# The prompt's layer-0 SwiGLU as seven block products, its moving operands streamed from DRAM through a ring

## The chip, the cores and the metric

The kernel runs on one core of one Trainium2 chip. The metric is device time of one execution in microseconds (us). The engines are TensorE (PE: matmuls, with the weight loads as a row of their own, PEld), VectorE (DVE), ScalarE (ACT), GpSimd (POOL) and SyncE (SP), which issues nearly all DMAs of this kernel from one queue, in order.

## The reference

Two residual layers run over two sequences, a prompt of 1024 tokens and a sample of 512, with the same weights. Layer 0 mixes tokens by a grouped Fourier transform, layer 1 by grouped-query attention (8 query heads, 2 key/value heads of 128); each is followed by a SwiGLU.

```python
def swiglu_ffn(x, g, w_gate, w_up, w_down):
    h = rms_norm(x, g)
    return (jax.nn.silu(h @ w_gate) * (h @ w_up)) @ w_down

def run_trunk(x):
    cos, sin = axial_rope_tables(x.shape[1])
    for i in range(DEPTH):                       # DEPTH = 2
        j = i // 2
        if i % 2 == 0:
            x = x + fourier_mixer(x, norm_mix[i], fourier_w[j])
        else:
            x = x + attention_mixer(x, norm_mix[i], attn_w_qkv[j], attn_q_norm[j],
                                    attn_k_norm[j], attn_w_o[j], cos, sin)
        x = x + swiglu_ffn(x, norm_ffn[i], ffn_w_gate[i], ffn_w_up[i], ffn_w_down[i])
    return x
```

The model width is 1024, the hidden width of the SwiGLU 2816. All is float32.

## The kernel before

Tokens are cut into three blocks of 512: block 0 is the sample, blocks 1 and 2 the prompt. Activations are kept transposed: a block is 8 chunks `dc` of 128 features by 512 tokens. Each float32 operand of a large product is split into a high part that TensorE multiplies exactly and a low rest, and `mm3` issues three matmuls for one product (high x high, high x low, low x high; lines 247, 248 and 249). ACT makes the high part (`act.copy`, a cast), VectorE or GpSimd the low one by a subtraction (`split`, lines 240 and 241; `weights`, lines 278 and 279). Residuals rest in DRAM (`xres`).

`ffn(layer, b, h)` is the SwiGLU of one block: for each of 22 chunks `fc` of the hidden width, 8 products for gate, 8 for up (into two `g` banks of PSUM), then silu, product and split into `mid`, and 8 products of the down projection, held in `pend` and issued one by one among the next chunk's. A down product goes to one of two `c` banks, and VectorE adds it to the accumulator (`acc`, line 750).

`ffn_pair(layer, blocks, ops, outs)` is the SwiGLU of two blocks at once, before the change for layer 1 only. Per pass it takes two hidden chunks f0 and f1, two halves of the contraction and two blocks, a 2x2 by 2x2 block product for gate and up, by seven block products and additions instead of eight (11 passes). A block product is 24 matmuls (two banks, gate and up; four feature chunks; three matmuls). Its stationary operands, sums and differences of weight blocks, come from `operands`/`stationary` (GpSimd adds at lines 924 to 930, then a split), its seven moving operands (B11, B21, T2, T1, B22, T3, N4: sums and differences of the normalised blocks) from `moving`. Five of these lie in SBUF (pool `mT`), two go to DRAM (`late`) and come back once into the slot `hA` before the pair needs them. Product banks: two tiles of two banks (`gT`, shown as `a`) and the two `g` banks, in turn. `plus` (line 915), `silu` and `hidden` empty them; 32 down products per pass go through `pend`.

`weave(main, main_cost, aux, aux_cost)` sets the order in which code is written out: a main stream (F) and an auxiliary one (X) are generators that yield costs, and the one that is behind in its share of its cost goes on; `lead` steps of the main stream come first. A scheduler then orders the instructions of each engine by that priority and by what it takes to be ready. Slots of tiles are given by tag (`BUFS`). The stages before, main and auxiliary:

1. `ffn(0, 0)` beside the prompt's Fourier mixer, its projection, and the norm of block 1
2. `ffn(0, 1)` beside the sample's attention (`qkv(0)`, `attend((0,))`) and the norm of block 2
3. `ffn(0, 2)` beside the sample's output projection, `qkv(1)`, and the norm of block 0
4. `ffn(1, 0)` beside `qkv(2)`, `attend((1, 2))`, two output projections and `moving`
5. `ffn_pair(1, (1, 2))` alone

## Time and profile before

| | |
|---|---|
| three runs | 3037.09 us median, 3036.11 to 3038.55 |
| profiled execution | span 3039.1 us, which is the time the profile gives for it |
| TensorE | 2965.8 us busy (98%), 14,184 matmuls |
| VectorE, ScalarE, GpSimd | 1660.7, 1235.4, 1283.2 us busy |
| DMA | 330.05 MB, mean 109 GB/s |
| mean granted TensorE clock | 0.995 of full speed |

Of these stages, 1 runs to about 530 us, 2 to 1043, 3 to 1533, 4 to 2350 and 5 to the end. A matmul's bar in the profile is longer than the distance to the next start, since matmuls overlap; what one costs is read from the starts, or from the number of matmuls in a window. Idle time counts only on TensorE or where it ends in a wait of TensorE. Tile names in the profile lack their digits: `B`, `T` and `late` are the moving operands, `a`, `g` and `c` PSUM banks.

### The profile page before, as it was taken

How to read it: one execution, taken by the hardware profiler on the slowest of the kernel's cores; microseconds unless marked ns; L12 is line 12 of the kernel's file. 1: busy time of each engine (PE TensorE's matmuls, PEld its weight loads, DVE VectorE, ACT ScalarE, POOL GpSimd, SP SyncE). 2: the span in 40 equal slices, each digit the busy share in tenths (PEclk: the TensorE clock that was granted, in tenths of full speed). 3: DMA queues.
4: the chain of work that ended last, by engine and by line, in shares of the span. 5: the costliest groups of instructions: out<-in, count | busy, mean ns of one | idle time of the engine just before them, and what ended most of it. 6: DMA issues, size and time to landing. Idle time of an engine off the chain costs nothing. (4 is left out here: it accounts for less than half of the span.)

```text
span 3039.1 us, 36901 instructions
## 1 busy us (share of the span) xinstructions
PE 2965.8 (98%) x14184; PEld 2434.2 (80%) x14184; DVE 1660.7 (55%) x2875; ACT 1235.4 (41%) x1843; POOL 1283.2 (42%) x652
## 2 busy tenths in 40 slices
PE   7999999999999999999999999999999999999999
PEld 6778888888877788888878788877787787887777
DVE  6785565534555543533473465665236555655566
ACT  6443232433466522333343577776324222222221
POOL 4434444433333644444433311313636644644452
PEclk9999999999999999999999999999999999999999
DMA  7434543332322734433343211212635411111111
GB/s 228 146 111 149 167 133 93 128 101 84 97 91 94 237 127 133 141 104 101 102 141 108 86 57 53 80 46 91 222 122 183 163 56 55 43 56 56 44 54 63
DMA packets 132080, 330.05 MB, mean 109 GB/s; under 512 B 14176, under 2 KB 28512, under 8 KB 131264
## 3 DMA queue, kind: packets, MB, share of 16 engines
q1 hardware_dynamic: 130688, 318.71, 32.2%
q0 software_dynamic: 928, 7.94, 0.7%
q8 instruction: 111, 1.82, 0.2%
q10 hardware_dynamic: 288, 1.05, 0.1%
q14 instruction: 65, 0.53, 0.1%
HBM read 280.45 MB, written 47.19 MB: 108 GB/s over the span
## 5 line engine op out<-in xcount | busy, mean ns | idle before, releaser
L279 POOL TENSOR_TENSOR w<-raw,w 128x1024 fp32r<-128x1024 f32 x354 | 847.5, 2405 | 1308.2 <-ACT w L278 1225.1
L750 DVE TENSOR_TENSOR acc<-c,acc 128x512 f32<-128x512 f32 x704 | 483.1, 689 | 443.4 <-PE c L249 439.1
L278 ACT CAST w<-raw 128x1024 fp32r<-128x1024 f32 x354 | 371.0, 1049 | 561.7 <-PE c L249 271.7
L247 PE MATMUL g<-h,w 128*128 128x512 f32 x1408 | 556.2, 395 | 3.6 <-ACT t L782 3.6
L249 PE MATMUL g<-h,w 128*128 128x512 f32 x1408 | 552.2, 392 | 0.5 <-POOL w L279 0.5
L248 PE MATMUL g<-h,w 128*128 128x512 f32 x1408 | 552.2, 392 | 0.0
L247 PE MATMUL c<-mid,w 128*128 128x512 f32 x1056 | 417.7, 397 | 15.5 <-DVE acc L750 10.8
L248 PE MATMUL c<-mid,w 128*128 128x512 f32 x1056 | 414.3, 392 | 1.7 <-DVE mid L241 1.7
L249 PE MATMUL c<-mid,w 128*128 128x512 f32 x1056 | 413.6, 392 | 0.0
L241 POOL TENSOR_TENSOR w<-raw,w 128x512 fp32r<-128x512 f32 (+1 forms) x178 | 239.8, 1370 | 310.5 <-ACT w L240 289.5
L863 DVE TENSOR_TENSOR acc<-c,acc 128x512 f32<-128x512 f32 x352 | 240.8, 689 | 186.3 <-PE c L249 185.5
L247 PEld LDWEIGHTS g<-h,w 128*128 128x128 f32 x1408 | 265.3, 188 | 56.7 <-ACT t L782 4.7
L249 PEld LDWEIGHTS g<-h,w 128*128 128x128 f32 x1408 | 265.3, 188 | 56.4 <-POOL w L279 1.6
L248 PEld LDWEIGHTS g<-h,w 128*128 128x128 f32 x1408 | 265.4, 189 | 51.9
L247 PEld LDWEIGHTS c<-mid,w 128*128 128x128 f32 x1056 | 198.2, 188 | 77.5 <-DVE acc L750 20.5
L248 PEld LDWEIGHTS c<-mid,w 128*128 128x128 f32 x1056 | 199.0, 188 | 41.9 <-DVE mid L241 3.7
L249 PEld LDWEIGHTS c<-mid,w 128*128 128x128 f32 x1056 | 198.6, 188 | 40.5
L248 PE MATMUL c<-h,w 128*128 128x512 f32 x480 | 188.2, 392 | 3.0 <-POOL h L241 2.9
L247 PE MATMUL c<-h,w 128*128 128x512 f32 x480 | 189.1, 395 | 0.0
L240 ACT CAST w<-raw 128x512 fp32r<-128x512 f32 (+1 forms) x178 | 107.6, 648 | 196.6 <-PE a L249 79.8
L249 PE MATMUL c<-h,w 128*128 128x512 f32 x480 | 187.0, 390 | 0.0
L1078 DVE TENSOR_REDUCE col<-a 128x1 f32<-128x1024 f32 (+1 forms) x96 | 100.4, 1046 | 127.9 <-PE a L249 127.6
(341 smaller groups left out, 4763.3 us busy)
## 6 DMA issues: line engine op xcount, KB each, us to landing
raw<-in_down_dram SPq DMA_DIRECT2D x110, 512.0 KB, 3.6
raw<-in_gate_dram SPq DMA_DIRECT2D x88, 512.0 KB, 3.5
raw<-in_up_dram SPq DMA_DIRECT2D x88, 512.0 KB, 3.7
raw<-in_qkv_dram SPq DMA_DIRECT2D x36, 512.0 KB, 3.9
t<-xres SPq DMA_DIRECT2D x56, 256.0 KB, 4.0
raw<-in_wo_dram SPq DMA_DIRECT2D x24, 512.0 KB, 3.7
raw<-in_gate_dram SPq DMA_DIRECT2D x44, 256.0 KB, 2.6
raw<-in_up_dram SPq DMA_DIRECT2D x44, 256.0 KB, 3.2
```

Of the source, the lines that this page charges most:

```text
L240: act.copy(hi, src)
L241: eng.tensor_tensor(lo, src, hi.bitcast(F32), op=ALU.subtract)
L247: pe.matmul(out, lh, rh, start=first, stop=False)
L248: pe.matmul(out, lh, rl, start=False, stop=False)
L249: pe.matmul(out, ll, rh, start=False, stop=last)
L278: pinned(act.copy(flat[:, 0], raw)) if early else act.copy(flat[:, 0], raw)
L279: pool.tensor_tensor(flat[:, 1], raw, flat[:, 0].bitcast(F32), op=ALU.subtract)
L750: dve.tensor_tensor(acc[dc], ps, acc[dc], op=ALU.add)
L863: dve.tensor_tensor(acc, ps, acc, op=ALU.add)
L1078: dve.tensor_reduce(st[:, 0:1], s_in, op=ALU.max, axis=AX.X)
```

## The change

- Layer 0's SwiGLU of the prompt becomes `ffn_pair` too. `ffn_pair` now takes a ring of eight pieces (slot `hB`) for moving operands, a table `places` of operands that stay in SBUF once fetched, and a flag `wide`.
- `moving` writes all seven operands to DRAM (`mov`, 28 stores of 512 KB), leaving B11 and B21 also in the ring. In `times` the loop over feature chunks is outside and the two banks inside, so that a piece (one chunk of one operand) is used for both banks and then released; `fetch` then issues the load of the piece eight places on. Layer 0 streams all seven operands in each pass; layer 1 keeps T1, B22, T3 and N4 in SBUF and streams the other three.
- The stages are now: `ffn(0, 0)` beside the prompt's mixer, projection and `moving`; the layer-0 pair beside the sample's `qkv(0)`, attention, output projection and norm; `ffn(1, 0)` beside `qkv(1)`, `qkv(2)`, the prompt's attention, two output projections and `moving`; the layer-1 pair alone. Beside the layer-0 pair the auxiliary stream is narrow: two PSUM banks in all, fewer buffers. That pair has one `gT` tile and the two `g` banks for its products (`wide` false), the one of layer 1 two and two as before.
- `ffn` asks for the next chunk's gate and up weights earlier (`want`).
- `qkv` of the sample and of block 2 reads the residual from DRAM again instead of the accumulators kept.

```diff
-        for fc in range(NF):
-            if here and fc == 0:
-                wg, wu, wd = (first[i] for i in range(3))
-            else:
-                wg, wu, wd = (weights(t[v][layer, fc]) for v in ("gate", "up", "down"))
+        for fc in range(NF):
+            want("gate", fc)
+            want("up", fc)
+            want("gate", fc + 1)
+            wg, wu = ready.pop(("gate", fc)), ready.pop(("up", fc))
...
+    def moving(blocks, gain, out, ring, helped):
...
+            x4 = tl("x", [2, 2, TB], F32, "wX")
...
+            def put(name, src):
+                if name in OPERANDS[:2]:
+                    x = ring[:, 4 * OPERANDS.index(name) + j]
...
+                split(x[:, 0], x[:, 1], src, eng=pool if name in helped else None)
+                sp.dma_start(out[name][:, j], x.bitcast(F32))
...
+    def ffn_pair(layer, blocks, ring, places, wide, outs):
...
+        order = [(v, j) for n in range(NF // 2) for v in OPERANDS if n == 0 or v not in places for j in range(4)]
+        pieces, turns = [ring[:, n] for n in range(8)], [0]
+        del order[:8]
+
+        def fetch():
+            if order:
+                v, j = order.pop(0)
+                if v in places:
...
+                else:
+                    x = ring[:, turns[0] % 8]
+                    turns[0] += 1
+                sp.dma_start(x.bitcast(F32), mov[layer][v][:, j])
+                pieces.append(x)
...
-        def times(w, x):
+        def times(w, name, f0):
             turn[0] += 1
-            if turn[0] % 3 == 0:
+            if turn[0] % (3 if wide else 2) == 0:
                 banks = [bankg(), bankg()]
             else:
                 g2 = tl("a", [2, TB], F32, "gT", gt)
                 banks = [g2[:, 0], g2[:, 1]]
-            for i in range(2):
-                for j in range(4):
-                    mm3(banks[i], w[:, 0, 4 * i + j], w[:, 1, 4 * i + j], x[:, 0, j], x[:, 1, j], j == 0, j == 3)
+            for j in range(4):
+                at_hand = name in places and f0 > 0
+                x = whole_[name][:, j] if at_hand else pieces.pop(0)
+                for i in range(2):
+                    mm3(banks[i], w[:, 0, 4 * i + j], w[:, 1, 4 * i + j], x[:, 0], x[:, 1], j == 0, j == 3)
                     some()
-                yield i, banks[i]
+                if not at_hand:
+                    fetch()
+                yield 2.2
+            return list(enumerate(banks))
...
+    def paired(layer, helped, places, wide, outs):
+        ring = h_slot("ring", F32R, "B")[:, 0 : 16 * TB].rearrange("p (s h n) -> p s h n", s=8, h=2)
+        yield from moving((1, 2), g_ffn[layer], mov[layer], ring, helped)
+        close_pool("sbX")
         close_pool("psX")
-        last["pair"] = ffn_pair(1, (1, 2), ops, t["y"])
+        last["pair"] = ffn_pair(layer, (1, 2), ring, places, wide, outs)
...
-    weave(ffn(0, 1, h_next), FFN_US, aux_1(), (QKV_US + 60.0) * SLACK, 9)
-    weave(ffn(0, 2, h_next), FFN_US, aux_2(), (LIN_US + QKV_US) * SLACK, 9)
-    weave(ffn(1, 0, h_next, t["y"][0]), FFN_US, aux_3(), FFN_US, 9)
+    narrow[0] = True
+    BUFS.update({"wX": 3, "rawX": 1, "ssX": 1, "pX": 1, "mT": 2, "gT": 1})
...
+    weave(last["pair"], 0.9 * PAIR_US, aux_1(), CHAIN_US, 24)
...
+    BUFS.update({"wX": 4, "rawX": 2, "ssX": 2, "pX": 2, "gT": 2})
...
+    weave(ffn(1, 0, h_next, t["y"][0]), 0.85 * FFN_US, aux_2(), PROMPT_US, 9)
     weave(last["pair"], 1.0)
```

How the order moves is shown at three places. First TensorE in layer 0's SwiGLU of the prompt, before, in `ffn(0, 1)` beside the sample's qkv projection (`c<-h` is the projection, `g<-h` gate or up, `c<-mid` a down product):

```order
L247 MATMUL c_5547<-h_4797,w_5544 128x512
L248 MATMUL c_5547<-h_4797,w_5544 128x512
L249 MATMUL c_5547<-h_4797,w_5544 128x512
L247 MATMUL g_5479<-h_3668,w_5470 128x512
L248 MATMUL g_5479<-h_3668,w_5470 128x512
L249 MATMUL g_5479<-h_3668,w_5470 128x512
L247 MATMUL c_5584<-mid_5460,w_5272 128x512
L248 MATMUL c_5584<-mid_5460,w_5272 128x512
L249 MATMUL c_5584<-mid_5460,w_5272 128x512
```

and now, in the layer-0 pair beside the same projection:

```order
L255 MATMUL g_6563<-ring_3385,w_6484 128x512
L256 MATMUL g_6563<-ring_3385,w_6484 128x512
L257 MATMUL g_6563<-ring_3385,w_6484 128x512
L255 MATMUL g_6564<-ring_3385,w_6484 128x512
L256 MATMUL g_6564<-ring_3385,w_6484 128x512
L257 MATMUL g_6564<-ring_3385,w_6484 128x512
L255 MATMUL c_6571<-mid_6481,w_6360 128x512
L256 MATMUL c_6571<-mid_6481,w_6360 128x512
L257 MATMUL c_6571<-mid_6481,w_6360 128x512
```

The moving operand is now a piece of the ring, used for both banks in turn from one stationary tile, with the down products between as before.

Second SP's queue in the same stage. Before, in `ffn(0, 1)` (`dot` is the sample's attention output on its way to DRAM):

```order
L274 DMA raw_9250<-in_wo_dram 128x1024
L274 DMA raw_7875<-in_up_dram 128x1024
L1108 DMA dot_97<-t_7704 128x256
L274 DMA raw_7880<-in_down_dram 128x1024
L1108 DMA dot_97<-t_7824 128x256
L274 DMA raw_8096<-in_gate_dram 128x1024
```

and now (`mov_B_99` is B11, `mov_B_100` B21, `mov_T_101` T2; `dqk` and `dot` belong to the sample's attention):

```order
L881 DMA ring_3385<-mov_B_99 128x1024 x3
L915 DMA raw_9415<-in_gate_dram 128x512
L881 DMA ring_3385<-mov_B_99 128x1024
L915 DMA raw_9415<-in_up_dram 128x512
L282 DMA raw_9538<-in_down_dram 128x1024
L1150 DMA dot_113<-t_9274 128x256
L881 DMA ring_3385<-mov_B_100 128x1024 x2
L1106 DMA raw_9713<-dqk_7_123 128x512
L881 DMA ring_3385<-mov_B_100 128x1024 x2
L282 DMA raw_9945<-in_down_dram 128x1024
```

Ring loads, each of which waits until TensorE has used the slot's last piece, now stand in the queue among the weights and the other stream's transfers.

Third SP's queue where the moving operands are formed. Before, in stage 4 (`x<-xres` are the residuals loaded for it):

```order
L809 DMA x_18638<-xres_92 128x512
L809 DMA x_18640<-xres_92 128x512
L809 DMA x_18642<-xres_93 128x512
L809 DMA x_18644<-xres_93 128x512
L809 DMA x_18790<-xres_92 128x512
L809 DMA x_18792<-xres_92 128x512
L274 DMA raw_18813<-in_gate_dram 128x1024
```

and now, beside `ffn(0, 0)`, from the stores of one group to the loads of the next:

```order
L845 DMA mov_T_102<-l_3867 128x1024
L282 DMA raw_3938<-in_down_dram 128x1024
L845 DMA mov_T_104<-l_3824 128x1024
L282 DMA raw_3975<-in_up_dram 128x1024
L845 DMA mov_T_101<-l_3930 128x1024
L845 DMA mov_N_105<-l_3930 128x1024
L828 DMA x_3991<-xres_95 128x512 x2
L828 DMA x_3991<-xres_96 128x512 x2
```

The loads of a group, which stood in the queue ahead of the stores of the one before, now stand behind its last store.

More of the change, by code (lines that the diff above doesn't have):

```diff
@@ L189, in bank, with thin @@
         return tl("c", [TB], F32, "c" + cur[0], pools["ps" + cur[0]])
+    narrow = [False]
+    def thin():
+        return narrow[0] and cur[0] == "X"
     def bank2():
@@ L197, in side @@
     def side():
-        return bankg() if cur[0] == "F" else bank2()[:, 0]
+        return bankg() if cur[0] == "F" else bank() if thin() else bank2()[:, 0]
     def sides():
@@ L315, in accumulators, with new_residual @@
         return [a[:, i] for a in halves for i in range(4)]
-    def new_residual(b, dc, piece, out=None, stays=False):
+    def new_residual(b, dc, piece, out=None, stays=False, room=None):
         if out is not None:
@@ L338, in normed @@
         r = in_rows(rstd[b])
+        if thin():
+            r, seen = tl("r", [TB], F32, "ssX"), r
+            act.copy(r, seen)
         h = h_tile(ab)
@@ L341, in normed @@
         for dp in range(NC // 2):
-            for dc, ps in zip((2 * dp, 2 * dp + 1), sides()):
+            for dc, ps in zip((2 * dp, 2 * dp + 1), (None, None) if thin() else sides()):
                 if held is None:
@@ L756, in one, with want @@
                 pend.pop(0)()
+        ready = {(v, 0): first[i] for i, v in enumerate(("gate", "up", "down"))} if here else {}
+        def want(v, fc):
+            if fc < NF and (v, fc) not in ready:
+                ready[v, fc] = weights(t[v][layer, fc])
         for fc in range(NF):
-            if here and fc == 0:
-                wg, wu, wd = (first[i] for i in range(3))
-            else:
-                wg, wu, wd = (weights(t[v][layer, fc]) for v in ("gate", "up", "down"))
+            want("gate", fc)
+            want("up", fc)
+            want("gate", fc + 1)
+            wg, wu = ready.pop(("gate", fc)), ready.pop(("up", fc))
             ga, up = bankg(), bankg()
@@ L786, in ffn @@
             pend.extend(lambda dc=dc, m=m, wd=wd, fc=fc: down(m, wd, fc, dc) for dc in range(NC))
-        while pend and layer == 1 and b == 2:
-            one()
-    def moving(blocks, gain, ops):
-        tp = open_pool("tT")
+    def moving(blocks, gain, out, ring, helped):
         yield 2.0
-        r = [in_rows(rstd[b], lambda n: tl("t", [n], F32, "tT", tp)) for b in blocks]
+        r = [in_rows(rstd[b]) for b in blocks]
         yield 1.0
         for j in range(4):
+            x4 = tl("x", [2, 2, TB], F32, "wX")
             v = {}
@@ L864, in down @@
             if fc == NF - 1:
-                new_residual(b, dc, acc, outs[b][:, dc, :])
+                new_residual(b, dc, acc, None if outs is None else outs[b][:, dc, :], room=spare)
         def some():
@@ L874, in quarter @@
         def quarter(fc, half):
-            raw = tl("raw", [2, TB], F32, "rT", raws)
+            raw = tl("raw", [2, TB], F32, "rT", raws) if fc or half else first_raw
             for i in range(2):
@@ L972, in ffn_pair @@
             wd1 = weights(t["down"][layer, f1])
-            for i, ps in step("T3"):
+            for i, ps in (yield from step("T3")):
                 plus(U[i], ps, U[i])
@@ L979, in ffn_pair @@
                     hidden(ps, s, f1, blocks[1], wd1)
-            for i, ps in step("N4"):
+            for i, ps in (yield from step("N4")):
                 plus(ps, ps, U[i])
@@ L994, in qkv @@
         got = {}
[L995 removed]
+        yield from normed(b, g_mix1, got, "ABB"[b], held)
         h = got["h"]
@@ L1070, in scores @@
                     qs = slice(qc * P, (qc + 1) * P)
-                    sc = bank2()
+                    sc = bank().unsqueeze(1) if thin() else bank2()
                     for kb in range(nb):
@@ L1088, in turned @@
                     if qc % 2 == 0:
-                        pts[qc // 2] = [acc_tile("pt", [2, 4, 256], F32R) for _ in range(nk // 4)]
+                        pts[qc // 2] = [w_tile(2, 4, 256) if thin() else acc_tile("pt", [2, 4, 256], F32R) for _ in range(nk // 4)]
                     pt = pts[qc // 2]
@@ L1202, in prepare @@
     def prepare(b, layer):
-        yield from normed(b, g_ffn[layer], nxt, "B" if b == 2 else "A")
+        yield from normed(b, g_ffn[layer], nxt, "A")
     def h_next():
@@ L1254, in aux_3 @@
+        yield from attend((1, 2))
+        for b in (1, 2):
+            yield from out_projection(b, "B")
         close_pool("ap")
[L1255 to L1264 removed]
@@ new lines, in late @@
+    def late():
+        if not late_:
+            two = h_slot("late", F32R, "A")[:, 0 : 16 * TB].rearrange("p (k c h n) -> p k c h n", k=2, c=4, h=2)
+            late_.extend([two[:, 0], two[:, 1]])
+        return late_.pop(0)
+    narrow[0] = True
+    BUFS.update({"wX": 3, "rawX": 1, "ssX": 1, "pX": 1, "mT": 2, "gT": 1})
+    open_pool("sbX", **RIGHT)
+    open_pool("psX", **RIGHT, **PS)
+    ap = open_pool("ap", **RIGHT)
+    weave(last["pair"], 0.9 * PAIR_US, aux_1(), CHAIN_US, 24)
+    for name in ("ap", "sbX", "psX"):
+        close_pool(name)
```

181 lines of the change are left out of this document (91 added, 90 removed).

## The prediction, made before the change was run

> **What bounds the kernel now.** I read the head of the page first, for the busiest engine, then its slices, for a stretch in which another engine or the DMA leads, then TensorE's starts one by one in the layer-1 pair, for the price of a matmul, and last the windows and waits of the stages that the change touches.
>
> ```profile
> span 3039.1 us, 36901 instructions
> PE 2965.8 (98%) x14184; PEld 2434.2 (80%) x14184; DVE 1660.7 (55%) x2875; ACT 1235.4 (41%) x1843; POOL 1283.2 (42%) x652
> PE   7999999999999999999999999999999999999999
> PEclk9999999999999999999999999999999999999999
> GB/s 228 146 111 149 167 133 93 128 101 84 97 91 94 237 127 133 141 104 101 102 141 108 86 57 53 80 46 91 222 122 183 163 56 55 43 56 56 44 54 63
> ```
>
> TensorE is busy in every slice but the first, at the full granted clock; no other engine is above 55%, and no slice moves more than 237 GB/s. The 98% does not say how long a matmul takes, because matmuls overlap; the starts do:
>
> ```profile
> 2499.84 0.39 PE L247 MATMUL c<-mid,w 128*128 128x512 f32 x1
> ...
> 2509.36 0.39 PE L247 MATMUL a<-B,w 128*128 128x512 f32 x1
> ```
>
> Between these rows lie 42 intervals in 9.52 us, so a 128x512 matmul costs 0.2267 us when nothing waits, and not the 0.39 us of its own bar. Against that pitch the windows show where time is lost:
>
> ```profile
> 400.00:450.00 50.00, 48.00 (x208) 39.24 (x207) 32.75 (x51) 17.08 (x23) 18.16 (x8) 0.97 0.39 129
> 1000.00:1100.00 100.00, 97.33 (x428) 79.14 (x429) 55.65 (x92) 41.18 (x56) 55.43 (x27) 1.00 0.56 188
> 1100.00:1200.00 100.00, 100.00 (x443) 82.81 (x442) 35.72 (x52) 26.03 (x33) 42.99 (x18) 1.00 0.40 134
> 1500.00:1600.00 100.00, 98.14 (x439) 78.15 (x438) 65.27 (x119) 42.57 (x63) 40.75 (x17) 1.00 0.40 130
> 2250.00:2400.00 150.00, 142.25 (x616) 113.34 (x616) 85.04 (x141) 51.67 (x85) 86.92 (x55) 0.99 0.55 189
> 2400.00:3000.00 600.00, 596.97 (x2583) 479.80 (x2583) 349.63 (x529) 154.27 (x254) 317.68 (x198) 1.00 0.15 49
> 2360.00:2380.00 20.00, 18.97 (x82) 14.92 (x82) 10.78 (x16) 5.65 (x10) 16.56 (x12) 1.00 1.01 373
> ```
>
> An FFN of one block beside other work (1100 to 1200) loses nothing: 443 matmuls in 100 us are 0.2257 us each. The pair (2400 to 3000) needs 0.2323 us each, 14 us over the pitch in 600 us. The handover into the pair (2250 to 2400) has 616 matmuls, about 136 us at their pitches (some 32 of them short ones), so it loses about 14 us; the handover at 400 to 450 has 208, 16 of them short, and loses about 5 us. The two others (1000 to 1100 and 1500 to 1600, mixed sizes) have TensorE idle for 2.7 and 1.9 us.
>
> **The change, part by part.** *Matmuls removed.* Per two feed-forward chunks and two blocks, gate and up take 7 products of 24 matmuls instead of 8 times 24; over 11 passes that is 264 matmuls of 128x512 fewer (12,997 rows on TensorE against 13,261, no other kind changes in number). They are on the path, since TensorE is: 264 x 0.2267 = -59.9 us.
>
> *The pair's own losses, now in layer 0 too.* The two FFNs that it replaces ran at the bare pitch; if 2,904 matmuls of layer 0 (168 + 96 per pass) took the pair's 0.2323 us, that would be +16 us. What is behind it:
>
> ```profile
> PE g L249 <- POOL w L241: 1.5, 3, 0.5
> PE a L249 <- POOL w L241: 1.5, 3, 0.7
> L241 POOL TENSOR_TENSOR w<-raw,w 128x512 fp32r<-128x512 f32 x138 | 175.4, 1296 | 185.1 <-ACT w L240 185.1
> L240 ACT CAST w<-raw 128x512 fp32r<-128x512 f32 x137 | 78.2, 620 | 163.3 <-PE a L249 69.4 <-PE c L249 61.9 <-PE g L249 25.4
> ```
>
> Part of it is waits for a stationary operand that ACT and POOL split late, because its slot came free late (ACT waits for PE). A split takes 2 x (0.62 + 1.30) = 3.8 us. Counting matmuls between the release of a slot and its next use, times the pitch, the new order leaves 7.5 us at least in layer 0 and 6.6 us in layer 1; the order before leaves 1.0 us at least. So these waits should go, and with them some of the switching between products. I take half, +8 us (0 to +16), for layer 0, and -3 us (-6 to 0) for layer 1, whose pair has the waits shown. The product now runs both banks side by side, so both halves of a stationary are needed at its start; the 7.5 us covers that.
>
> *The ring.* In layer 0 the queue order has 220.2 MB from the first to the last ring transfer. TensorE's work there is 834 us at the pitch, some 860 us with losses, so 256 GB/s, above every slice shown. What stands for it: the window of 2360 to 2380 moved 373 GB/s. A slot is refilled after its piece is used, and needed 7 pieces later: 10.2 us at least, 21 us in the median, by the count of matmuls between. Landings:
>
> ```profile
> raw<-in_down_dram SPq DMA_DIRECT2D x110, 512.0 KB, 3.6
> raw<-in_qkv_dram SPq DMA_DIRECT2D x36, 512.0 KB, 3.9
> x_p<-in_rows_p_dram SPq DMA_DIRECT2D x8, 512.0 KB, 6.3
> ```
>
> 3.6 us, and 6.3 us in the crowd of the start, both lie inside 10.2 us, so the ring costs TensorE 0. Not covered in that way are the loads of the other stream (about 20 weights and 40 smaller ones beside the pair): in engines that work in order, each that lands later than the order assumes holds what is queued behind. Bound: 0, if all have room; 60 x (6.3 - 3.6) = +160 us, if none has; nearest is the row of FFN beside projections, where nothing is lost at 134 GB/s, so I take +5 us (0 to +40). The traffic of layer 1's pair rises from 49 GB/s to about 160, its ring slack is 15.6 us at least: 0.
>
> A page of the Trainium skill speaks against this step: "DMA: Bandwidth & Descriptors", sections "Rules for kernel authors" and "Bandwidth", asks for at least 1 MiB per DMA and measures 341 GB/s for 1 MB and 138 for 64 KB. The pieces are 512 KB; an estimate half way between these two figures would be 240 GB/s, and 220.2 MB would take 918 us, 58 us over my 860, which would take back the whole gain. The window at 373 GB/s, made of 512 KB and larger transfers, disagrees, so the sum keeps 0.
>
> *Accumulators and product banks in layer 0.* Two product buffers of two banks instead of three. Draining the longest step (T3) takes VectorE four adds, a product and a subtraction and ACT a cast:
>
> ```profile
> L863 DVE TENSOR_TENSOR acc<-c,acc 128x512 f32<-128x512 f32 x315 | 215.8, 690 | 175.3 <-PE c L249 174.4
> L915 DVE TENSOR_TENSOR a<-a,t 128x512 f32<-128x512 f32 x38 | 26.5, 697 | 19.8 <-PE a L249 19.0
> L241 DVE TENSOR_TENSOR mid<-a,mid 128x512 fp32r<-128x512 f32 x25 | 17.1, 685 | 1.4 <-ACT mid L240 0.7
> ```
>
> 4 x 0.70 + 0.69 + 0.59 + 0.69 = 4.8 us, up to 8.2 us with five accumulations of 0.69 between. After T3 the new order has 8.8 us at least, in the median over all steps 12.1 us. Cost 0, thin; it is a rival below.
>
> *Moving operands and handovers.* Forming the operands ran once and now runs twice, with 28 stores more each time on SP's queue. What it did:
>
> ```profile
> 2292.63 0.76 DVE L814 SCALAR_TENSOR_TENSOR a<-x,gains,c 128x512 f32<-128x512 f32 x1 [3.04 <-DMA x<-xres]
> ...
> 2324.96 0.75 DVE L814 SCALAR_TENSOR_TENSOR x<-x,gains,c 128x512 f32<-128x512 f32 x1 [3.19 <-DMA x<-xres]
> PE c L247 <- DVE acc L750: 5.6, 4, 2.7
> ```
>
> VectorE stood before loads that SP issued late, the FFN's accumulations stood behind it, and TensorE ran out of c banks (5.6 us). The loads of the next group still stand behind the stores of the last, so I charge 5.6 us again beside layer 0's first FFN, 0 for the transfers themselves (the DMA has room). Handovers: before, four (5 + 2.7 + 1.9 + 14 = 24 us); after, three: into the layer-0 pair 3 (759 FFN matmuls, 172 us, follow the last projection there, so it is like the two small ones), into layer 1 3, into the layer-1 pair 12 (225 FFN matmuls, 51 us, between the last output projection and the pair's first product, against 327, 74 us, before; but more buffers for the operands on their way out, so I leave it near the 14). 5.6 + 18 - 24 = 0 us (-14 to +12).
>
> *Attention.* The order has as many matmuls between two score groups of the prompt as before (median 4.8 us), so its 11.7 us of waits stay:
>
> ```profile
> PE a L247 <- ACT p L1082: 11.7, 8, 1.8
> ```
>
> The sample's has more cover (209 against 159 us between its groups) and one bank less: 0 (-5 to +5). The FFN's earlier prefetch of gate and up removes nothing, since the FFN waits for no weights.
>
> Sum against the profiled execution: 3039.1 - 59.9 + 8 - 3 + 5 + 0 = 2989.2 us. That span is 2.0 us above the median of the three runs (3037.09), which spread over 2.4 us; so 2987 us.
>
> **Rivals.** *SP's queue blocks the ring* (slower). In the layer-1 pair SP stood up to 16.3 us before one transfer that needs a weight slot; behind it were only weights, now ring pieces are.
>
> ```profile
> SPq L878 <- POOL w L241: 329.1, 36, 16.3
> ```
>
> 16.3 + 3.6 - 12 us of slack in the lean steps is 8 us, once in each of 11 passes 87 us: 3074 us. It decides from 4.6 us per pass on (50 us in all). Against it: SP stood so long because it ran ahead; the ring holds it to TensorE's pace, where these slots are free.
>
> *The DMA cannot keep 256 GB/s.* At the 237 GB/s of the best slice, layer 0 needs 929 us, 69 more: 3056 us. For it: no slice is higher. Against it: 373 GB/s for 20 us, and slices were low for want of demand. The rule of the Trainium skill's page "DMA: Bandwidth & Descriptors" quoted above would act like this.
>
> *Product banks drain late.* If each of layer 0's 77 products waited 0.4 us: +31 us, 3018 us. For it: 8.8 us against 8.2, with the other stream's work also on VectorE. Against it: that is the least gap, and VectorE is 58% busy in the pair.
>
> *All losses go.* No premium in layer 0, handovers at their best, nothing late: 2987 - 8 - 14 - 5 = 2960 us.
>
> That the products are not removed is excluded by the instruction count.
>
> **How the numbers follow.** Forecast (2963 to 3002) 0.69; banks late, around 3018, 0.13; all losses go, 2950 to 2963, 0.10; SP blocked 0.04; DMA too slow 0.04. A measurement tells 0.2%, 6 us, from no change. The last two, when mild, end within it (0.03) and otherwise slower (0.05); all else is faster, 0.92. The range of 2957 to 3016 leaves out 0.2: half of the banks' case (0.065), half of the best (0.05) and the slow ones (0.08).
>
> **What will show it.** Right: TensorE at about 13,920 matmuls (264 fewer), pitch of the layer-0 pair under 0.232 us, 230 to 270 GB/s there, hardly any idle TensorE put down to ring transfers, DVE drains of a or g under 10 us in sum. Wrong: TensorE idle on DMA ring in each pass, SP waiting for POOL with ring transfers landing late, or waits of VectorE for loads that grow beside the layer-0 pair; and a larger loss around the two formings of operands than the 18 us charged.

## The result: slower, 3070 us instead of 2987

The changed kernel takes 3069.79, 3070.37 and 3078.82 us (one more execution, of twice the time, is left out as disturbed); against the kernel before its ratio is 1.0117, 95% interval 1.0101 to 1.0133. The forecast was 2987 us (2957 to 3016). The profile is of the execution of 3078.82 us, the slowest of the three, so what is counted in it below holds some 8 to 9 us that the other two do not lose.

The head of the changed kernel's page and its slices:

```profile
span 3077.0 us, 37570 instructions
PE 2953.5 (96%) x13920; PEld 2415.3 (78%) x13920; DVE 1804.1 (59%) x3049; ACT 1237.4 (40%) x1929; POOL 1337.6 (43%) x746
PE   7999989989999999999899999999997999999999
PEclk8999999999999999999999999999998999999999
GB/s 222 140 103 171 138 266 169 254 235 250 238 247 244 246 235 280 273 250 197 189 116 108 103 62 66 66 52 59 187 169 265 341 166 162 137 138 200 141 137 89
```

The 264 matmuls are gone (13,920 against 14,184), and the span is 37.9 us longer. Some slices of PE and two of PEclk are lower than before. The same in windows (span of a window, then busy time and count of PE, PEld, DVE, ACT, POOL, then granted clock, DMA share and GB/s):

```profile
350.00:560.00 210.00, 197.02 (x878) 159.54 (x877) 146.02 (x224) 70.51 (x99) 105.38 (x50) 0.98 0.54 187
560.00:720.00 160.00, 146.82 (x614) 115.71 (x613) 96.95 (x145) 51.17 (x86) 69.18 (x41) 0.94 0.79 267
720.00:1200.00 480.00, 476.38 (x2267) 392.85 (x2266) 288.36 (x512) 220.55 (x370) 219.18 (x137) 1.00 0.73 246
1430.00:1560.00 130.00, 117.69 (x504) 92.77 (x503) 86.62 (x140) 56.26 (x82) 48.86 (x20) 0.95 0.51 170
2280.00:2500.00 220.00, 197.16 (x795) 152.48 (x794) 125.52 (x179) 62.23 (x102) 115.55 (x69) 0.93 0.70 256
2500.00:3050.00 550.00, 549.99 (x2407) 449.36 (x2406) 327.35 (x493) 140.15 (x236) 290.47 (x182) 1.00 0.41 145
```

The layer-0 pair beside attention (720 to 1200) and the layer-1 pair (from 2500) run as they should: 2407 matmuls in 550 us are 0.2285 us each, better than the 0.2323 of before. The time is lost around them: where the operands are formed (350 to 560, 2280 to 2400), where a pair starts (560 to 720, 2400 to 2500), and where it hands over (1430 to 1560).

To put numbers on it I took every TensorE start of the two traces and subtracted from each window the matmuls in it at their pitches (0.2267 us for 512 columns, about half for 256 and fewer). What is left is TensorE's loss, stalls and half clock together. Windows of different kernels do not hold exactly the same work, but the sums fit the spans: 97.6 us more loss less 59.9 us of matmuls are 37.7 us, against the 37.9 us between the spans. The last three columns are experiments below; their stages end some tens of us earlier.

| window, us | before | changed | h_base | i_late | j_pace16 |
|---|---|---|---|---|---|
| 0 to 350, start, mixer | 36.4 | 47.5 | 40.3 | 41.7 | 36.1 |
| 350 to 560, forming, layer 0 | 5.1 | 20.5 | 9.0 | 10.2 | 10.6 |
| 560 to 720, start of its pair | 1.4 | 26.0 | 20.6 | 10.5 | 10.1 |
| 720 to 1200, pair beside attention | 16.3 | 11.6 | 12.6 | 14.9 | 15.6 |
| 1200 to 1430, output projection, norm | 1.7 | 11.7 | 17.5 | 12.6 | 11.1 |
| 1430 to 1725, handover, qkv | 14.7 | 25.9 | 19.1 | 19.8 | 23.8 |
| 1725 to 2150, attention of the prompt | 30.6 | 29.2 | 31.4 | 31.5 | 31.6 |
| 2150 to 2280, output projections | 1.5 | 13.3 | 10.8 | 11.4 | 11.0 |
| 2280 to 2500, forming and start, layer 1 | 15.3 | 43.1 | 21.9 | 21.0 | 15.0 |
| 2500 to the end, pair | 16.3 | 8.1 | 7.7 | 7.8 | 7.6 |
| sum | 139.3 | 236.9 | 190.9 | 181.4 | 172.5 |
| half-clock spells (below) | 4 | 22 | 14 | 11 | 13 |

TensorE's longest groups of waits in the changed kernel, and the ring's transfers (count, size, median us to landing):

```profile
PE c L255 <- ACT mid L248: 13.2, 8, 2.6
PE c L255 <- DVE acc L900: 12.0, 12, 3.2
PE c L255 <- DVE acc L762: 11.6, 10, 3.4
PE a L255 <- ACT p L1124: 8.3, 6, 1.6
PE a L257 <- POOL w L249: 7.3, 6, 2.6
PE c L316 <- ACT t L315: 4.6, 1, 4.6
```

```profile
ring<-mov_B SPq DMA_DIRECT2D x204, 512.0 KB, 5.1
ring<-mov_T SPq DMA_DIRECT2D x176, 512.0 KB, 5.6
```

No wait of TensorE ends with a ring transfer in this profile. TensorE waits for accumulations that free a `c` bank (the two `acc` rows, 23.6 us, against 11.2 in the kernel before), for the split of `mid` (13.2 against 3.7), and for stationaries (`w`), that is for VectorE, ACT and GpSimd, although none of these is busy above 70% in any of the windows shown. The last row is not new: the kernel before has the same wait with 4.7 us.

**Why VectorE is late: a lock.** VectorE and GpSimd in the layer-0 forming:

```profile
431.43 5.20 POOL L287 TENSOR_TENSOR w<-raw,w 128x1024 fp32r<-128x1024 f32 x2 [4.75 <-ACT w L286]
```

```profile
431.36 0.68 DVE L802 TENSOR_TENSOR g<-g,ss 128x512 f32<-128x512 f32 x1
431.95 2.42 DVE L856 TENSOR_TENSOR x<-x 128x512 f32<-128x512 f32 x1
434.30 2.88 DVE L249 TENSOR_TENSOR l<-x,l 128x512 fp32r<-128x512 f32 x1
437.11 0.69 DVE L803 TENSOR_TENSOR g<-g,ss 128x512 f32<-128x512 f32 x1
```

```profile
439.67 0.50 PE L255 MATMUL c<-mid,w 128*128 128x512 f32 x1 [2.56 <-ACT mid L248]
```

A VectorE instruction of 128x512 takes 0.68 us when one input is in PSUM (`g`). The two with both inputs in SBUF (`x<-x`, `l<-x,l`) take 2.42 and 2.88 us, each until about the end of one of GpSimd's two instructions of 2.6 us. Behind them stood the products for `mid`, and TensorE stood 2.56 us for it. Two SBUF inputs alone are not slow: by starts and ends in this trace, 16 of the 32 differences `x<-x` ran while GpSimd was idle and took 0.67 to 0.68 us each, while the 16 beside a working GpSimd took up to 2.86 us, 1.66 in the median. Nor is a working GpSimd alone: 535 accumulations `acc<-c,acc`, with one input in PSUM, ran beside it and none took over 0.70 us. Before, the differences of the forming were kept in PSUM (`a`), so none of this was in the forming's trace. The Trainium skill's page "SBUF — State Buffer", section "SBUF: two separate sides", states it: VectorE and GpSimd share a port pair under an exclusive lock, which a VectorE instruction with two SBUF inputs needs while GpSimd reads SBUF, and the loser blocks for the whole instruction. The trace agrees, 0.68 us against 2.4 to 2.9.

**Why a short stall costs more than itself: the clock.** Windows of 5 us around a stall of 3.2 us:

```profile
625.00:630.00 5.00, 5.00 (x23) 3.92 (x22) 4.22 (x7) 0.59 (x1) 0.19 (x1) 1.00 0.93 298
640.00:645.00 5.00, 1.79 (x7) 1.15 (x6) 4.95 (x4) 0.00 (x0) 3.12 (x2) 0.86 0.26 59
645.00:650.00 5.00, 5.00 (x13) 3.93 (x12) 2.64 (x5) 0.74 (x2) 0.00 (x0) 0.50 0.95 315
```

After the stall the granted clock is 0.50, and 13 matmuls start in 5 us instead of 22 or 23. The changed kernel has 22 such spells (130 us in all, each a multiple of 3.4 us), the kernel before 4 (27 us). Matmuls in them start 0.427 us apart, so they cost 0.2 us more each: about 43 us of the 237 lost, against 8 of 139. A stall is counted here from start to start, less the pitch. Of the 21 stalls of 2 us and more after the first 60 us, 16 were followed by a spell within 7 us; of the 21 spells after that time, six had no such stall close before them, only shorter ones, so the length of one stall does not decide alone. The Trainium skill's page "TensorE: Matmul & The Clock Gate", section "HAM oscillation — how this bites in real kernels", warns of idle gaps over about 3.4 us; here stalls of 2.0 to 2.1 us were followed by a spell in some cases (at 83, 608 and 2188 us).

### The profile page after: what moved, and what is told of

The parts are those of the page before. It is cut to its first block, busy times and chain, and to the rows that moved or that the text cites. A ratio compares the mean times of both kernels' runs of the same rounds, so it can differ in the third digit from the quotient of the medians.

```text
span 3077.0 us, 37570 instructions
## 1 busy us (share of the span) xinstructions
PE 2953.5 (96%) x13920; PEld 2415.3 (78%) x13920; DVE 1804.1 (59%) x3049; ACT 1237.4 (40%) x1929; POOL 1337.6 (43%) x746
## 4 chain that ended last, share of the span: by engine, by line
PE 74%; DVE 6%; DMA 4%; POOL 3%; issue 3%; ACT 2%; SPq 0%; POOLq 0%; ACTq 0%; DVEq 0%
PE c L255 11%; PE c L256 11%; PE c L257 11%; PE a L255 6%; PE a L257 6%; PE a L256 6%; PE g L257 6%; PE g L256 6%; PE g L255 6%; PE c L1138 2%; POOL w L287 2%; DMA raw<-in_down_dram 1%; DVE col L1121 1%; DMA t<-dot 1%; POOL w L249 1%
## 5 line engine op out<-in xcount | busy, mean ns | idle before, releaser
L287 POOL TENSOR_TENSOR w<-raw,w 128x1024 fp32r<-128x1024 f32 x244 | 587.3, 2415 | 1022.8 <-ACT w L286 999.9
L249 POOL TENSOR_TENSOR w<-raw,w 128x512 fp32r<-128x512 f32 (+1 forms) x332 | 437.3, 1341 | 511.7 <-ACT w L248 498.1
L255 PE MATMUL c<-mid,w 128*128 128x512 f32 x1056 | 424.8, 406 | 39.5 <-ACT mid L248 13.2
L257 PE MATMUL c<-mid,w 128*128 128x512 f32 x1056 | 418.4, 396 | 2.8 <-POOL w L287 2.8
L286 ACT CAST w<-raw 128x1024 fp32r<-128x1024 f32 x244 | 255.3, 1049 | 411.6 <-issue 121.5
L256 PE MATMUL c<-mid,w 128*128 128x512 f32 x1056 | 418.9, 397 | 1.1 <-DVE mid L249 0.9
L248 ACT CAST w<-raw 128x512 fp32r<-128x512 f32 (+1 forms) x332 | 197.3, 635 | 388.1 <-PE a L257 158.2
L257 PE MATMUL g<-h,w 128*128 128x512 f32 x704 | 282.7, 402 | 5.8 <-POOL w L287 5.8
L255 PE MATMUL g<-h,w 128*128 128x512 f32 x704 | 282.9, 402 | 5.5 <-ACT t L804 4.8
L256 PE MATMUL g<-h,w 128*128 128x512 f32 x704 | 281.7, 400 | 1.8 <-DVE h L252 1.8
L255 PE MATMUL a<-ring,w 128*128 128x512 f32 x488 | 193.7, 397 | 6.1 <-DVE x L831 4.2
L257 PE MATMUL a<-ring,w 128*128 128x512 f32 x488 | 192.4, 394 | 3.0 <-POOL w L249 2.9
L256 PE MATMUL a<-ring,w 128*128 128x512 f32 x488 | 192.0, 393 | 0.0
L255 PEld LDWEIGHTS g<-h,w 128*128 128x128 f32 x704 | 135.9, 193 | 36.2 <-ACT t L804 6.6
```

Of the source, the lines that this page charges most:

```text
L248: act.copy(hi, src)
L249: eng.tensor_tensor(lo, src, hi.bitcast(F32), op=ALU.subtract)
L255: pe.matmul(out, lh, rh, start=first, stop=False)
L256: pe.matmul(out, lh, rl, start=False, stop=False)
L257: pe.matmul(out, ll, rh, start=False, stop=last)
L286: pinned(act.copy(flat[:, 0], raw)) if early else act.copy(flat[:, 0], raw)
```

## Experiments

Ratios are to the kernel before, run beside each on the same chip (medians 3035.6 to 3037.3 us there). The groups f, g, h with i, and j ran on different chips, so across groups the ratios compare better than the times.

**f_psum, f_norm, f_all, b_sbuf: the lock.** f_psum keeps the operands' differences in PSUM again:

```diff
+            a2 = bank2()
+            a, b = a2[:, 0], a2[:, 1]
...
-            dve.tensor_tensor(v[0, 0], v[0, 1], v[0, 0], op=ALU.subtract)
-            put("T1", v[0, 0])
+            dve.tensor_tensor(b, a, v[0, 0], op=ALU.subtract)
+            put("T1", b)
```

> The changed kernel, but the differences that form the moving operands are kept in PSUM again (one factor of each subtraction), on the same engines; in layer 1 no VectorE instruction of the forming has two SBUF inputs any more, in layer 0 twelve subtractions still have. Port theory (a VectorE instruction with two SBUF inputs stands still while GpSimd works): the stretched instructions (1.1 to 2.2 us in the mean) fall to 0.69 us, TensorE's loss at 2290 to 2500 us falls from 43 to 15 to 25 us and at 350 to 500 us from 20 to about 14, the time by 15 to 30 us to 3045 to 3058 us. Load theory (VectorE and ACT stand before residuals that SP loads late behind the stores): the waits for loads are untouched, the time stays within 6 us of the changed kernel's 3070. Density theory (too much VectorE work pressed into too short a stretch, whatever its operands): also within 6 us.

Measured: 3053.7 us, ratio 1.0047 (1.0032 to 1.0062), 17 us under the changed kernel by the medians, 21 by the ratios. Groups of the layer-1 forming (2260 to 2410 us; count | busy, mean ns), changed kernel first, then f_psum:

```profile
L249 DVE TENSOR_TENSOR l<-x,l 128x512 fp32r<-128x512 f32 x8 | 9.1, 1153 | 0.0
L856 DVE TENSOR_TENSOR x<-x 128x512 f32<-128x512 f32 x4 | 9.0, 2238 | 1.3 <-POOL l L249 1.2
```

```profile
L249 DVE TENSOR_TENSOR l<-a,l 128x512 fp32r<-128x512 f32 x8 | 5.5, 684 | 1.7 <-ACT l L248 1.7
L858 DVE TENSOR_TENSOR a<-x,a 128x512 f32<-128x512 f32 x4 | 2.7, 686 | 0.0
```

The same work takes 0.69 us again where it took 1.15 and 2.24 (the slowest of the four groups of differences; the others took 0.84 to 1.34). With it went TensorE's waits: from 350 to 560 us, for `mid` from ACT 7.0 us became 2.0, for accumulations 4.1 became 1.0. The loss of 350 to 500 us fell to 10 (expected 14), that of 2280 to 2500 us only to 35 (expected 15 to 25), so something else is in it.

b_sbuf does the opposite to the kernel before: the four differences in SBUF.

```diff
-            dve.tensor_tensor(b, a, v[0, 0], op=ALU.subtract)
-            put("T1", b)
+            dve.tensor_tensor(v[0, 0], v[0, 1], v[0, 0], op=ALU.subtract)
+            put("T1", v[0, 0])
```

> The kernel before, but the four differences of the forming of the moving operands have both inputs in SBUF, as in the changed kernel; the number and order of loads, stores and matmuls stay. Port theory: these instructions (16 subtractions and 8 splits, 0.69 us each) stretch to 1 to 2 us, the loss at 2250 to 2400 us rises from 13 to 20 to 35 us, the time by 6 to 20 us to 3043 to 3057 us. Load and density theories: no change, within 4 us of 3037.

Measured: 3053.0 us, ratio 1.0047 (1.0032 to 1.0062), 16 us slower by the medians. In its profile, of the fastest of its four executions (3048.9 us), the loss of 2250 to 2400 us rose from 13 to 23 us. Two of its groups in the forming, which took 0.69 us each before:

```profile
L241 DVE TENSOR_TENSOR T<-x,T 128x512 fp32r<-128x512 f32 x8 | 10.7, 1340 | 0.0
L835 DVE TENSOR_TENSOR x<-x,x 128x512 f32<-128x512 f32 x4 | 7.4, 1858 | 0.0
```

With both directions, and with the same instruction at 0.68 us beside an idle GpSimd, the lock is shown: same instructions, same engines, only the operand's place differs. f_norm takes the lock out of the norm and of the squares beside the layer-0 pair (row factor in PSUM, low halves and the adding of squares to GpSimd):

```diff
+                    dve.scalar_tensor_tensor(x, x, gain[:, dc : dc + 1], r, op0=ALU.mult, op1=ALU.mult)
+                    split(h[:, 0, dc], h[:, 1, dc], x, eng=pool)
...
-            dve.tensor_tensor(ss[b], sq, ss[b], op=ALU.add)
+            (pool if room else dve).tensor_tensor(ss[b], sq, ss[b], op=ALU.add)
```

> The changed kernel, but beside the layer-0 pair the norm keeps its row factor in PSUM and GpSimd takes the low halves of its split, and GpSimd adds the squares of the new residuals; so the VectorE instructions with two SBUF inputs of the stages from 560 to 1530 us are gone. Port theory: the loss at 560 to 690 us falls from 26 to under 12 us, that of 1430 to 1560 us from 21 to 10 to 15, the time by 15 to 30 us to 3045 to 3058 us. Load theory (the sample's residuals stand behind ring loads on SP's queue, ACT's casts of the stationaries behind them): losses there unchanged, time within 6 us of 3070. Cost of the added GpSimd work, if it makes the stationaries later: up to 10 us slower.

Measured: 3069.8 us, ratio 1.0111 (1.0095 to 1.0127): no gain that shows, so the port theory's forecast failed here. The loss of 560 to 720 us fell from 26 to 18, that of 1430 to 1560 us stayed (22.4 of 23.2). A likely reading, not tested, is that instructions stretched by the lock cost time only where TensorE waits for VectorE next.

> Both edits together, and in layer 0 GpSimd takes the low halves of B22, T3 and N4 as it does in layer 1, so that VectorE has no instruction with two SBUF inputs in the formings and norms. Port theory: the two gains add up, 3010 to 3035 us, below the kernel before; half-clock spells fall from 23 to about 10. Load and density theories: 3060 to 3075 us.

f_all (both, and GpSimd on five of seven low halves in layer 0): 3041.9 us, 1.0022 (1.0007 to 1.0037), better than f_psum by 12 us in the medians, but above the 3010 to 3035 expected; 14 half-clock spells besides the last. Which of its two additions gave the 12 us is not separated.

**g_side, g_lead, g_defer, g_best: the other places.** At 83 us TensorE stood 1.9 us in the changed kernel, where the one before stood 0.7, and a half-clock spell followed at 84 us. (The 5.06 us at 78 us in the expectation below do not stand in the trace.) TensorE at that place, before and changed:

```profile
78.14 0.36 PE L247 MATMUL c<-eo,w 128*128 128x258 f32 x1 [0.68 <-DVE acc L715]
```

```profile
83.28 0.36 PE L255 MATMUL c<-eo,w 128*128 128x258 f32 x1 [1.86 <-DVE acc L727]
```

ACT some us earlier, before and changed:

```profile
67.29 0.60 ACT L329 ACTIVATE a<-acc 128x512 f32<-128x512 f32 x1 [1.85 <-DVE acc L711]
```

```profile
71.21 0.60 ACT L337 ACTIVATE g<-acc 128x512 f32<-128x512 f32 x1 [1.92 <-DVE acc L723]
```

The diff's `side()` puts the squares of new residuals into a `g` bank, one of two that the projection weights pass through there. g_side puts them back:

```diff
-            sq = room() if room else side()
+            sq = room() if room else bank2()[:, 0] if "psX" in opened and not narrow[0] else side()
```

> The changed kernel, but the squares of new residuals go to the auxiliary stream's double bank again as long as that pool is open (before: a<-acc; changed: g<-acc, into one of the two banks that the weights of the sample's projection need). Bank theory for the start: the stall of 5.06 us at 78 us falls to the 0.97 us of before, TensorE's loss from 0 to 350 us from 47.5 to 36 to 40 us, the half-clock spells there from 4 to 1 or 2, the time by 6 to 12 us to 3058 to 3064. If the start differs only by when its first loads land: no change, 3066 to 3078.

Measured: 3064.2 us, 1.0092 (1.0077 to 1.0107), 6 to 8 us off, though its interval and that of the changed kernel just overlap; the stall is 0.7 us again (at 82 us) and the half-clock spells at 84 and 115 us are gone. The loss to 350 us is 42.1 and not 36 to 40, since the first spell, at 26 us, lasted 23.9 us in this execution and 13.7 in the kernel before. Its length does not hang on the edits: j_pace16 and j_pace22, alike up to there, have 13.7 and 23.9.

g_lead lets layer 1's SwiGLU of the sample run ahead (`weave(..., PROMPT_US, 24)` for `9`).

> The changed kernel, but in stage 3 layer 1's SwiGLU of the sample runs 24 steps ahead of the other stream instead of 9, so that qkv of block 1 starts later behind the end of the layer-0 pair. Chain theory (the last residuals, their squares, the norm factor and the normalised block must pass VectorE and ACT before TensorE's first qkv product, which stands in TensorE's order ahead of matmuls that are ready): the loss of 1430 to 1560 us falls from 23 to under 12 us, the time by 8 to 15 us to 3056 to 3064. If that loss is VectorE being full at the pair's end (adds of the last 16 down products and squares), it stays above 18 us and the time within 5 us of 3070.

Measured: 3096.9 us, 1.0195 (1.018 to 1.021), 24 us slower: a miss for both. The loss of 1430 to 1560 us stayed at 24.8, so the chain theory in that form fell, and 2400 to 2500 us lost 31.3 instead of 10.7. After the last output projection 126 matmuls of that SwiGLU's gate and up are left, against 201 in the changed kernel; the start of the layer-1 pair then stands bare and waits for its stationary:

```profile
PE a L255 <- ACT w L248: 11.1, 2, 8.3
```

g_defer is f_psum with each store of a moving operand written one step later, and the next group's residuals asked for earlier:

```diff
-                sp.dma_start(out[name][:, j], x.bitcast(F32))
+                stores.append((out[name][:, j], x.bitcast(F32)))
...
+            flush()
+            if j < 3:
+                coming = fetched(j + 1)
             yield 5.0
```

> f_psum, and each store of a moving operand is written one step later, the residuals of the next group are asked for ahead of half of the stores. Queue theory (SP stands before a store whose operand VectorE or GpSimd has not finished, and the FFN's weights and the next residuals stand behind it): against f_psum (3054) another 8 to 20 us off, to 3034 to 3046; the losses of 350 to 500 us (10 in f_psum) and 2280 to 2500 us (35) fall to 5 and to 18 to 25. Port theory alone: what is left of these losses in f_psum is density and the start of the pair, no change, 3049 to 3059.

Measured: 3045.5 us, 1.0027 (1.0015 to 1.0039), 8 us under f_psum; 2280 to 2500 us lost 22 instead of 35, but 350 to 500 us 20 in this profile (10 in f_psum). The two intervals overlap, and the cause is not shown: of TensorE's waits from 2280 to 2500 us, those for stationaries of the pair and most of those for accumulations went, but the one for a gate weight, which later stores should have shortened, grew from 5.6 to 12.2 us.

> The changed kernel with the differences in PSUM, GpSimd on five of seven low halves in both layers, the squares in the auxiliary bank, the lead of 24, and the later stores: if the four causes add up, 20 + 5 + 9 + 11 + 13 us off 3070: 3005 to 3020 us, 0.6 to 1% under the kernel before. If they share one loss, 3030 to 3040.

g_best: 3064.9 us, 1.0098 (1.0081 to 1.0114); the lead spoils it (49 us lost from 2280 to 2500 us).

**h_base, h_noacc, h_drain12, h_lin: what is left.** h_base is g_best without the lead.

> The changed kernel with the differences in PSUM, GpSimd on five of seven low halves in both layers, the squares in the auxiliary bank and the later stores, with the lead of 9 as it was. Each cause on its own term: 20 (differences) + 7 (squares) + 8 (stores) + about 4 (low halves) off 3070: 3026 to 3036 us. If the terms share losses: 3036 to 3046.

Measured: 3032.8 us, 0.9987 (0.9973 to 1.0001): level with the kernel before, 38 us under the changed one. The terms add up, 39 against 38, but the 4 us of the low halves were never measured alone.

> h_base, but the pairs' sums start from the first down product alone: the residuals are left out of both pairs' results and their 32 loads out of SP's queue, the number of VectorE instructions stays. Queue theory for the start of the pair (weights of the first stationaries stand behind accumulator loads and ring loads): the loss of 560 to 720 us falls from about 22 to under 12 us, the time by 10 to 20 us under h_base. If that loss is the filling of the chain of stationaries and the sample's norm: within 5 us of h_base.

```diff
             if fc == 0:
-                sp.dma_start(acc, xres[b][:, dc, :])
-            dve.tensor_tensor(acc, ps, acc, op=ALU.add)
+                dve.tensor_copy(acc, ps)
+            else:
+                dve.tensor_tensor(acc, ps, acc, op=ALU.add)
```

Measured: 3018.2 us, 0.9942 (0.9921 to 0.9963), 15 us off; the loss of 560 to 720 us 10.4 instead of 20.6. In h_base SP there takes turns between `acc<-xres` and ring pieces, and the weights come after; TensorE's waits for stationaries at 560 to 700 us in h_base, all three absent in h_noacc:

```profile
PE g L257 <- POOL w L249: 3.4, 2, 2.5
PE a L257 <- POOL w L249: 2.4, 1, 2.4
PE a L255 <- ACT w L248: 1.9, 1, 1.9
```

h_drain12 leaves the pair's last down products to the next stage (`while pend and outs is not None`). With its lead of 12 steps qkv of block 1 begins before they are done, and takes the norm factor of the residual before: its sums and that dependency are left out there.

> h_base, but the last down products of the layer-0 pair are not written out at its end: layer 1's SwiGLU of the sample issues them one by one among its first products, as other stages do, and runs 12 steps ahead. VectorE theory (at the pair's end accumulations, squares, the last products and the sample's norm come at once): the loss of 1430 to 1560 us falls from 22 to 8 to 14 us, the time by 8 to 14 us. Chain theory (the norm factor of block 1 is needed at once by qkv, wherever the last products stand): it stays at 18 to 25, or grows, since the last products come later: time within 5 us of h_base or up to 10 above.

Measured: 3031.7 us, 0.9982 (0.9971 to 0.9992). The handover's loss (1430 to 1560) fell from 16.2 to 6.5, but the time by 1 us: 2150 to 2500 us lost about 6 more, most of it in one wait for a weight (15.7 us, against 12.4 in h_base). That the last products and the norm chain make this loss is shown only with that part left out.

h_lin asks for each output projection's residual one step earlier (`x, coming = coming, wanted(n + 1)`).

> h_base, but each output projection asks for its residual one column block earlier. Load theory for 1200 to 1300 and 2150 to 2280 us (VectorE stands up to 5.5 and 10.9 us before these residuals, accumulations behind it): these losses fall from 8 and 12 us to 2 to 4 and 4 to 7 us, the time by 8 to 15 us under h_base. If the stalls there come from the split of the attention output on GpSimd: within 4 us.

Measured: 3034.3 us, 0.9989 (0.998 to 0.9999), no gain; 2150 to 2280 us lost 10.6 against 10.8, so the load theory fell there. From 1200 to 1300 us the loss was 7.7 against 11.8, but i_late, without this edit, has 6.1. TensorE waits for `h` from GpSimd in that window in the changed kernel (5.4 us in 6 waits), which was not pursued.

**i_late, i_drain, i_both: moving the work instead of leaving it out.** i_late starts the accumulators as copies and fetches one residual per block in each pass, added by GpSimd:

```diff
+            if fc == 2 * dc + 2:
+                x = tl("res", [TB], F32, "res", raws)
+                sp.dma_start(x, xres[b][:, dc, :])
+                pool.tensor_tensor(acc, x, acc, op=ALU.add)
```

> h_base, but the accumulators of the pairs start as copies of the first down product, and their residuals (the same 32 loads) come one per block in each pass, added by GpSimd. Place theory: the loss of 560 to 720 us falls from 21 to about 10 as without these loads, the time by 8 to 15 us under h_base, to 3018 to 3026. If it is the loads as such, or 32 more GpSimd instructions of 1.3 us delay the stationaries: within 4 us of h_base (3033) or above.

Measured: 3022.0 us, 0.9954 (0.9939 to 0.9968); 560 to 720 us lost 10.5. It was the place of these loads, not the loads.

> h_base, but the last down products of the layer-0 pair are issued among the first products of layer 1's SwiGLU of the sample, and qkv of block 1 begins when its norm factor is there. Place theory: the loss of 1430 to 1560 us falls from 16 to 6 to 9 us, the time by 4 to 10 us under h_base. Cover theory: what is gained there is lost at 2280 to 2500 us, where that SwiGLU then has fewer matmuls left beside the forming of the operands (as with the lead of 24): within 4 us of h_base, or above.

i_drain: 3040.9 us, 1.0015 (1.0003 to 1.0027), 8 us slower than h_base: 2 us gained at the handover, 10 lost at 2280 to 2500 us. It came as the cover theory said: 171 of that SwiGLU's gate and up matmuls are left after the last output projection, against 201. The largest wait there is again the one for a gate weight (15.5 us against 12.4).

> Both edits on h_base. If the places add up: 3008 to 3022 us, 0.5 to 1% under the kernel before. If the cover is what counts: 3018 to 3030.

i_both: 3022.1 us, 0.9952 (0.9938 to 0.9965), no better than i_late.

**j_pace16, j_pace22: the version that beats both.** In i_late one wait was left (TensorE, 2280 to 2400 us), and SP's queue shows it:

```profile
PE g L255 <- ACT w L286: 12.1, 1, 12.1
```

```profile
2291.95 3.39 SPq L837 DMA_DIRECT2D mov_T<-l  x3
2297.61 0.32 SPq L837 DMA_DIRECT2D mov_N<-l  x1
2297.99 0.43 SPq L282 DMA_DIRECT2D raw<-in_gate_dram  x1
```

TensorE needed this gate weight at 2293 us; SP asked for it at 2298. From 2260 us on it had issued no weight, only the stores and residual loads of the forming, three groups of them; the rows show the last stores. j_pace16 lets a step of the layer-1 forming count 1.6 times, so that more of the SwiGLU is written between:

```diff
-        yield from moving((1, 2), g_ffn[layer], mov[layer], ring, helped)
+        for v in moving((1, 2), g_ffn[layer], mov[layer], ring, helped):
+            yield v * (1.6 if layer else 1.0)
```

> i_late, but the steps of layer 1's forming count 1.6 times as much, so that more of the SwiGLU (265 matmuls between the last output projection and the pair's first, against 189) stands between them. Queue theory: the gate weight is asked for in time, the stall of 12.3 us goes, the loss of 2280 to 2500 us falls from 21 to 8 to 14 us, the time by 6 to 13 us to 3009 to 3016. Cover theory: the 24 matmuls of the SwiGLU left beside the pair's start, against 72, lose it again there: 3018 to 3026.

Measured: 3014.8 us, 0.9933 (0.9921 to 0.9946), the fastest: about 20 us under the kernel before and 55 under the changed one. Its interval and that of i_late overlap a little; 2280 to 2500 us lost 15.0 instead of 21.0. Of the wait of 12.1 us 4.6 are left (on a down weight).

> The same with 2.2: 309 matmuls before the pair's first, none left beside its start. Queue theory: as j_pace16, 3009 to 3016. Cover theory: the start of the pair stands bare, 5 to 15 us slower than j_pace16.

j_pace22: 3017.2 us, 0.9939 (0.9923 to 0.9954), the same within the intervals; the bare start cost nothing here, so bareness alone does not explain the loss of g_lead.

## Why the prediction was wrong, point by point

- *Matmuls removed*, -59.9 us: right, 264 fewer at an unchanged pitch.
- *The pair's own losses*: as forecast or better. +8 was charged for layer 0; 720 to 1430 us, the pair beside attention and output projection, lost 23.3 us, against 18.0 in that window before, and 1300 to 1430 us, the pair almost alone, 0.6. Layer 1's pair gained 8 (3 forecast): its waits for late stationaries, 2.8 us from 2500 us on before, went, as the count of matmuls said; the rest of the 8 is not assigned.
- *The ring*, 0: right. 246 GB/s over 480 us, and landings of 5.1 to 5.6 us in the median, 9.9 at most, inside the 10.2. One support for it was misread: the window at 373 GB/s before the change was not made of 512 KB and larger transfers. 56% of its bytes came in 2 MB transfers to `late`, and nearly all of the other transfers were of 256 KB, so that argument came out right by luck. The changed kernel's own window at 2400 to 2450 us moved 371 GB/s in pieces of 512 and 256 KB. The rule of the Trainium skill's page "DMA: Bandwidth & Descriptors", section "Rules for kernel authors" (1 MiB per DMA), did not decide.
- *Loads of the other stream*, +5 (0 to 40): the wrong loads. The residuals of the output projections cost nothing measurable (h_lin); the accumulators' loads at a pair's start, of which the prediction said nothing, cost 10 to 11 (i_late; they fall into the window of the next point).
- *Moving operands and handovers*: the step that failed. It charged 5.6 + 18 us against 24 before, 0 in sum. The windows 350 to 720, 1430 to 1725 and 2280 to 2500 us lost 115.5 us, against 36.5 in the same windows before: 79 us, of the 87.8 by which the span passed the sum of 2989.2. The prediction named this sign of being wrong, a larger loss around the two formings, but gave it no case among its rivals. What the runs took off, about: 20 us with the differences back in PSUM (f_psum, and b_sbuf the other way). This is the lock, which the diff shows (`x` in place of `a` and `b`) and the prediction overlooked: it priced the forming by the waits of a trace in which these instructions took 0.69 us. 10 to 11 us with the accumulators' loads spread over the passes (i_late). 6 to 8 us with later stores and earlier residual loads (g_defer), a place that the prediction named but sized by the waits of before, and where the cause is not shown. 6 to 7 us with the pace in layer 1 (j_pace16 against i_late). In j_pace16, which has all of these, the same windows lose 59.5 us: 56 of the 79 us are gone, 23 stay.
- *Not in the prediction at all*: the bank of the squares at the start, 6 to 8 us (g_side), and the half clock, which is part of the losses above. It sized each stall by its own length; the trace before had four half-clock spells, at 409 and 2328 us just behind the stalls that it priced, and a spell of 3.4 or 6.8 us costs 1.6 or 3.2 us (8 or 16 matmuls at 0.2 us).
- *Rivals*: none of the slower ones was what happened. SP blocked weights, not the ring; product banks did not drain late. The range's upper end of 3016 is close to what j_pace16 reaches.
- Open: j_pace16 still loses 33 us more than the kernel before, mostly in five windows with 5 to 10 us each (350 to 560, 560 to 720, 1200 to 1430, 1430 to 1725, 2150 to 2280). For the handover the chain behind the pair's last products is shown only with part of it left out; moving it gained nothing. For the output projections no cause is shown. About 5 of the 11 us that the start loses more than before in these two profiles are the longer first spell, which is chance.

## What to carry to other kernels

Removing work from the bound engine pays only if the engines that feed it keep their place: check each instruction that changes its operands' memory, not only its engine and count, and look for VectorE instructions with two SBUF inputs beside a busy GpSimd. Price a stall of 2 us or more on TensorE with the half-clock spell that may follow it (16 of 21 here), and give each forming enough independent matmuls beside it. Where one queue carries stores, weights and residuals, the order in the queue decides when a stage can start; a load that can come any time belongs where the queue is idle.

## What the runs showed of the hardware that was not expected

- A 128x512 subtraction on VectorE: 0.68 us with an input in PSUM, or beside an idle GpSimd; with both inputs in SBUF beside a working GpSimd up to 2.9 us, in means of a group 0.84 to 2.24. 24 such instructions cost 16 us of the whole time by the medians (b_sbuf), 10 of them seen in the window of the forming.
- The clock fell to 0.50 22 times in one execution, once for 23.9 us near the start and then for 3.4, 6.8 or 10.2 us; 16 of 21 stalls from 2.0 us on were followed by such a spell.
- Transfers of 512 KB and less held 246 GB/s for 480 us, and 366 GB/s for 10 us at 600 us, without one wait of TensorE that ends with a ring piece.
